# Differential attention: a filler's sums moved from VectorE to ScalarE and GpSimd, and one masked eviction for a row's last chunk

## The chip, the cores and the metric

The kernel runs on one core of one Trainium2 chip. A core has five engines with queues of their own: TensorE (PE in the profile; PEld are its weight loads), VectorE (DVE), ScalarE (ACT), GpSimd (POOL) and SyncE (SP, which issues nearly all DMAs here). The metric is the device time of one execution in microseconds. Lower is better. One execution was also taken with the hardware profiler; its trace is what the profile shows.

## The reference

Two transformer layers over 2048 tokens of width 1024, in float32. The first mixes three kinds of attention (six heads of stick-breaking attention, six of differential attention, four of attention to a memory of 256 tokens), the second has windowed attention and memory attention. Each layer ends in a gated product with `w_out` and a layer norm of `ALPHA * x + y`. The parts that the change touches:

```python
DEEPNORM_ALPHA = (2 * DEPTH) ** 0.25            # ALPHA in the kernel, the square root of 2

def _differential_attention(q, k, v, lam):
    ...
    s = jnp.einsum('bqhcd,bkhcd->bhcqk', qi, k) * scale
    causal = key_idx[None, :] <= q_idx[:, None]
    p = jax.nn.softmax(jnp.where(causal, s, NEG_BIG), axis=-1)
    a = p[:, :, 0] - lam * p[:, :, 1]
    return jnp.einsum('bhqk,bkhd->bqhd', a, v)

def _even_layer(x, mem, positions, ...):
    ...
    mixed = jnp.concatenate([sb_o, df_o, mem_o], axis=-1)
    y = (mixed * jax.nn.silu(gate)) @ w_out
    return _layer_norm(DEEPNORM_ALPHA * x + y, ln_g, ln_b)
```

## The kernel before

`run` goes through stages one after the other: `layer1_proj` (projections), `stick_breaking`, `differential`, `join` (the first layer's output product and norm), then `layer2_kv`, `layer2` and a last `out_proj`. Each stage has pools of SBUF tiles with a fixed number of buffers for each tag, and PSUM banks likewise. Matmuls of float32 are split into a high and a low part.

**Differential attention** works on 24 units: head pair `p` (3), half `k` (2), step `j` (4). `diff_parts` pairs a long row of query blocks with a short one, so that each unit has 17 blocks of 128 key columns: part `w = 0` with 9 to 16 of them, part `w = 1` with 1 to 8. For each of four score maps (`hc`: two heads, two maps each) `chunk` computes scores in chunks of up to 512 columns. A matmul writes a bank `psz` (three buffers), and VectorE evicts it into the SBUF tile `row` times `-scale`, and takes the minimum of a row on the way (`mn`, which the exponential needs). The last chunk of a part holds the diagonal block and needs the causal mask. One instruction, `tensor_tensor_reduce` (L779; CUSTOM_DVE_ANT_0 in the profile, ISA in the lists of order), adds the mask from the SBUF tile `mask`: zeros, then the triangle. The mask has two blocks of zeros, so that instruction reaches 384 columns. A last chunk of 512 columns is evicted in two pieces: 128 columns with the plain form (L777, TENSOR_SCALAR_CACHE_REDUCE), then 384 with the mask, starting from the first piece's minimum. That is so in part 0 where `j = 0` and in part 1 where `j = 3`: 3 x 2 x 2 x 4 = 48 chunks.

Then ScalarE takes exponentials in place (`exps`), VectorE forms the factors (L808, L812) and mixes two maps (`mix`, L819: `row` times a factor plus `row`, in three pieces). PE transposes the mixture (`pstp`), ScalarE copies the transposes into `wT` tiles (`tblocks`, a ring of seven buffers), and PE multiplies them with the values (`pspv`). `diff_norm` normalises a finished block of rows; its power (L895) and product (L897) run on GpSimd.

**The filler.** Beside all this, `filler` already computes five of the eight row blocks of the first layer's output product, in 32 blocks (two halves of columns, 16 blocks of rows). For each: `resid` loads 512 columns of `x` into `rx`, `split` splits the inputs (ScalarE, and GpSimd in L947), `products` issues 15 matmuls into the only bank `psmm`, and `finish` (L958) adds `ALPHA * x` to the product on VectorE and stores the sum to `rp`. The steps are spread evenly between the steps of attention. `join` loads `rp`, adds the last three row blocks of the product (L1063, in `out_proj`, with `alpha` None) and applies the norm.

**What sets the order.** In `differential` PE and ScalarE keep the program's order (`PinnedCore`). VectorE, GpSimd and SP are ordered by a scheduler that runs a timeline of its own when the kernel is built. On every engine, and on SP, the queue is then worked off in that order: what waits holds up what stands behind it.

Of the kernel before, what the change touches and what calls it, by code (L numbers as in the profile page):

```python
# [9 lines left out]
BF16 = mybir.dt.bfloat16  # L10
I32 = mybir.dt.int32
AF = mybir.ActivationFunctionType
ALU = mybir.AluOpType
# [53 lines left out]
class Net:  # L67
# [60 lines left out]
    def consts(self):  # L128
# [5 lines left out]

        self.mask = sb.tile([P, 3 * P + 2], BF16, name="mask")
        nc.vector.memset(self.mask[:, :2 * P], 0.0)
        nc.vector.memset(self.mask[:, 3 * P:], NEG)
        self.load_mask(2, 2)
        self.freq = sb.tile([P, 2], F32, name="freq")
# [406 lines left out]
    def stick_breaking(self):  # L546
# [33 lines left out]
        def scores(u):  # L580
            p, t, qi, c = u
            n, lo, hi = bounds(u)
            m, diag, s0 = hi - lo, hi == n, int(lo == 0)
            if qi == 3 and c == t:
                begin(p, t)
            if c == t:
                prs[p, t, qi] = [self.t("row", F32, [P, 2048]) for _ in range(2)]
                for hh in range(2):
                    nc.gpsimd.memset(prs[p, t, qi][hh][:, n - 1:n], 1.0)
            z = self.psum("z", [P, 2, 512])  # L590
            for hh in range(2):
                for k in range(2):
                    self.nc.tensor.matmul(z[:, hh, :m], qs[p, t][:, hh, k, qi * P:(qi + 1) * P], kv[p][0][hh][:, lo:hi], start=(k == 0),
                                          stop=(k == 1 and not diag))
                if diag:
                    self.nc.tensor.matmul(z[:, hh, m - P:m], self.identb, self.mask[:, 2 * P + 1:3 * P + 1], start=False, stop=True)
            zs[u] = z
# [144 lines left out]
    def diff_scores(self, unit, rows):  # L742
# [15 lines left out]
        def chunk(hc, w, c):  # L758
# [15 lines left out]
            before = mn[:, :1] if w and c else 3e38  # L774
            acc, n0 = mn[:, c:c + 1], max(0, m - 3 * P) if diag else m
            if n0:
                nc.vector.tensor_scalar(e[:, col + lo:col + lo + n0], z[:, :n0], -scale, before, ALU.mult, ALU.min, accum_out=acc)  # L777
            if diag:
                nc.vector.tensor_tensor_reduce(e[:, col + lo + n0:col + hi], z[:, n0:m], self.mask[:, 3 * P + n0 - m:3 * P], -scale,  # L779
                                               acc if n0 else before, ALU.add, ALU.min, acc)  # L780
            if w and c == 0:
# [130 lines left out]
    def filler(self):  # L912
# [43 lines left out]
        def finish(f):  # L956
            h, tb = blocks[f]
            self.nc.vector.scalar_tensor_tensor(res[f], res[f], ALPHA, res["ps"], ALU.mult, ALU.add)  # L958
            self.dma(self.rp[tb, :, 512 * h:512 * h + 512], res[f])
# [69 lines left out]

    def out_proj(self, w, msrc, spans, res, alpha, lng, lnb, tbs, ahead):  # L1030

# [19 lines left out]
        for k, tb in enumerate(tbs):  # L1051
# [7 lines left out]
            for h in range(2):  # L1059
                hs = slice(h * 512, h * 512 + 512)  # L1060
                ps = self.out_mm(mp, w, hs)
                if alpha is None:
                    nc.vector.tensor_add(r[:, hs], r[:, hs], ps)  # L1063
                else:
                    nc.vector.scalar_tensor_tensor(r[:, hs], r[:, hs], alpha, ps, ALU.mult, ALU.add)  # L1065
                nc.vector.bn_stats(st[:, 6 * h:6 * h + 6], r[:, hs])  # L1066
# [5 lines left out]
            nc.vector.scalar_tensor_tensor(r, r, mvr[:, 0:1], g, ALU.subtract, ALU.mult)  # L1072
            if alpha:
                for hs in (slice(0, 512), slice(512, 1024)):
                    nc.vector.scalar_tensor_tensor(r[:, hs], r[:, hs], rs, b[:, hs], ALU.mult, ALU.add)  # L1075
            else:
                nc.scalar.mul(r, r, rs)
                nc.gpsimd.tensor_add(r[:, :640], r[:, :640], b[:, :640])
                nc.vector.tensor_add(r[:, 640:], r[:, 640:], b[:, 640:])
            yield tb, r  # L1080

    def join(self, tail):
# [10 lines left out]
        raws[0] = self.t("big")  # L1093
        blocks = self.out_proj(w, self.m1, ((3, 6),), self.rp, None, i["ln_ge"], i["ln_be"], tbs, 2)

# [79 lines left out]
    def swa_scores(self, qb, head, qs, qcol, ks):  # L1175
# [12 lines left out]
        for hh in range(2):  # L1188
            nc.vector.tensor_tensor_reduce(e[:, hh, n0:], z[:, hh, n0:], self.mask[:, P + n0:3 * P], -1.0, self.nsink[:, head + hh:head + hh + 1],
                                           ALU.add, ALU.min, nmx[:, hh:hh + 1])  # L1190
# [227 lines left out]
    def run(self):  # L1418
        nc, dr, i = self.nc, self.dr, self.i
        with self.phase({"c2": 3, "sl": 2}, {}):  # L1420
# [17 lines left out]
            with self.phase({"big": 16}, {}):  # L1438
# [7 lines left out]
                with self.phase({"w": 4, "raw": 1, "cs": 2, "e": 4, "wT": 4, "kc": 2, "qs": 2, "vg": 4},  # L1446
                                {"mm": 2, "z": 3, "tp": 2, "pv": 1}):
                    self.load_mask(1, 1)
                    w = self.layer2()
                with self.phase({"gb": 2, "m": 3, "mp": 5, "rx": 6}, {"mm": 8}):  # L1450
                    tbs = [4 * t + q for t in (3, 0, 1, 2) for q in range(3, -1, -1)]
                    self.nc = PinnedCore(nc, self.tc, ("tensor",))
                    for tb, r in self.out_proj(w, self.m2, ((0, 8),), self.x2, ALPHA, i["ln_go"], i["ln_bo"], tbs, 3):
                        n = D // 2 if tb == tbs[-1] else D
                        for c in range(0, D, n):
                            self.dma(self.out[tb][:, c:c + n], r[:, c:c + n], nc.scalar if c else None)
# [68 lines left out]
```

## Time and profile before

| | us |
|---|---|
| median of 3 runs | 2526.95 |
| lowest and highest of them | 2522.09, 2529.95 |
| the profiled execution | 2526.36 |
| its span in the trace | 2524.5 |
| stage of differential attention, from the first score's eviction to the last one's | about 1050 to 1572 |

The profile lists instructions by line and tile, busy times of the engines in a stretch, and waits with what ended them. A line of a helper stands for all who call it: in `differential` PE and ScalarE are wrapped, and their instructions are under L57, so tiles tell them apart: `psz` scores, `psmm` the filler's product, `pstp` transposes, `pspv` products with the values. In waits, "A <- B" means that A's engine stood idle until B was done.

### The profile page before, as it was taken

Reading aid. Unit: us, or ns where it says so; the run is one execution under the profiler, and the core shown is the slowest. Engines: PE = TensorE matmul, PEld = TensorE weight load, DVE = VectorE, ACT = ScalarE, POOL = GpSimd, SP = SyncE. Lnnn points to the kernel's source line nnn. Section 1 sums busy time; section 2 is a strip of 40 time slices with the busy share of each in tenths; the row PEclk is TensorE's granted clock in tenths of the full one; section 3 lists DMA queues with packets and bytes.
Section 4 is the critical chain, followed back from the end, with each engine's and each line's share of the span. In section 5 each row is a group of like instructions: output and inputs, shape, how many; then the busy total and the mean of one; then the engine's idle time right before and its main releaser. Section 6 shows DMA issues by size and latency. Waiting matters only on the chain. (4 is left out here: it accounts for less than half of the span.)

```text
span 2524.5 us, 42315 instructions
## 1 busy us (share of the span) xinstructions
PE 2390.9 (95%) x15564; PEld 1939.1 (77%) x15564; DVE 1572.5 (62%) x3689; ACT 1262.1 (50%) x2459; POOL 939.6 (37%) x768
## 2 busy tenths in 40 slices
PE   9999999999999999889888998899999999999998
PEld 7888998888877777667666676688788777777887
DVE  4532223542278988799899998684313676777455
ACT  4432222232167877668677777443212777776100
POOL 0401003750068778511111111564511655534332
PEclk9999999999999999999999999999999999999999
DMA  8543222342433436734552431553324555532641
GB/s 282 196 142 126 72 87 90 130 138 79 135 87 94 108 85 133 160 90 109 128 134 72 112 87 54 197 183 108 95 89 116 162 151 153 145 102 98 200 149 60
DMA packets 199247, 311.60 MB, mean 123 GB/s; under 512 B 17920, under 2 KB 97280, under 8 KB 198528
## 3 DMA queue, kind: packets, MB, share of 16 engines
q1 hardware_dynamic: 198464, 307.83, 41.2%
q8 instruction: 124, 2.03, 0.4%
q10 hardware_dynamic: 576, 1.05, 0.1%
q14 instruction: 83, 0.68, 0.1%
HBM read 204.74 MB, written 104.07 MB: 122 GB/s over the span
## 5 line engine op out<-in xcount | busy, mean ns | idle before, releaser
L57 PE MATMUL psmm<-big,w 128*128 128x512 f32 x1680 | 413.2, 393 | 0.0
L57 PEld LDWEIGHTS psmm<-big,w 128*128 128x128 f32 x1680 | 305.3, 188 | 57.5
L57 ACT COPY wT<-pstp 128x512 f32<-128x512 f32 (+3 forms) x400 | 203.5, 526 | 188.9 <-PE pstp L57 182.9
L612 POOL TENSOR_TENSOR wb<-wb,row 128x512 f32<-128x512 f32 (+3 forms) x240 | 263.2, 1120 | 70.5 <-DVE row L57 45.4
L57 DVE TENSOR_TENSOR_SCAN row<-s,row,pszero 128x512 f32<-128x512 f32 (+5 forms) x240 | 254.1, 1104 | 38.2 <-ACT s L57 34.6
L254 PE MATMUL psmm<-big,w 128*128 128x512 f32 x1200 | 275.2, 389 | 0.0
L254 PEld LDWEIGHTS psmm<-big,w 128*128 128x128 f32 x1200 | 225.0, 188 | 47.0 <-issue 0.2
L57 PE MATMUL psmm<-big,mp 128*128 128x512 f32 x1056 | 246.0, 393 | 3.4 <-POOL big L1017 3.4
L57 ACT ACTIVATE row<-row,mn 128x2048 f32<-128x2048 f32 (+7 forms) x192 | 229.8, 1202 | 11.5 <-DVE mn L783 7.6
L57 PEld LDWEIGHTS psmm<-big,mp 128*128 128x128 f32 x1056 | 199.1, 190 | 45.4 <-POOL big L1017 3.8
L777 DVE TENSOR_SCALAR_CACHE_REDUCE row<-psz 128x512 f32<-128x512 f32 (+1 forms) x324 | 200.6, 639 | 16.0 <-PE psz L57 15.3
L947 POOL TENSOR_TENSOR mp<-mp,mp 128x640 fp32r<-128x640 f32 x32 | 54.2, 1693 | 347.4 <-ACT mp L57 274.9
L1236 DVE TENSOR_TENSOR c<-psmm,c 128x512 f32<-128x512 f32 x62 | 42.7, 691 | 219.2 <-ACT c L1235 219.1
L57 PE MATMUL psmm<-wo,mp 128*128 128x512 f32 x480 | 148.3, 421 | 6.3 <-ACT mp L57 5.5
L819 DVE SCALAR_TENSOR_TENSOR row<-row,tiny,row 128x128 f32<-128x128 f32 (+7 forms) x144 | 152.6, 1110 | 0.4
L209 POOL TENSOR_TENSOR w<-w,w 128x1024 fp32r<-128x1024 f32 x20 | 48.6, 2429 | 251.3 <-ACT w L208 147.0
L57 PE MATMUL pstp<-ident,wb 128*128 128x128 f32 x816 | 117.3, 276 | 22.8 <-DVE wT L57 15.3
L57 PE MATMUL pstp<-ident,row 128*128 128x128 f32 x816 | 130.4, 281 | 7.8 <-ACT wT L57 6.8
L1235 ACT ACTIVATE c<-psmm 128x512 f32<-128x512 f32 x62 | 36.8, 596 | 189.2 <-PE psmm L254 173.1
L57 PEld LDWEIGHTS pstp<-ident,wb 128*128 128x128 f32 x816 | 91.8, 141 | 43.7 <-POOL wb L612 27.0
L1193 ACT ACTIVATE e<-e,tiny 128x256 f32<-128x256 f32 (+1 forms) x192 | 94.7, 494 | 60.6 <-DVE e L1191 60.1
L57 PEld LDWEIGHTS pstp<-ident,row 128*128 128x128 f32 x816 | 99.4, 143 | 32.5 <-ACT wT L57 14.0
(236 smaller groups left out, 5009.9 us busy)
## 6 DMA issues: line engine op xcount, KB each, us to landing
silu<-c SPq DMA_DIRECT2D x54, 256.0 KB, 2.3
sl<-silu SPq DMA_DIRECT2D x54, 256.0 KB, 3.3
qs<-sbq SPq DMA_DIRECT2D x48, 256.0 KB, 5.3
cs<-rope SPq DMA_DIRECT2D x24, 512.0 KB, 4.2
kc<-k SPq DMA_DIRECT2D x36, 320.0 KB, 5.0
w<-in_we_dram SPq DMA_DIRECT2D x20, 512.0 KB, 3.7
raw<-in_wo_dram SPq DMA_DIRECT2D x20, 512.0 KB, 3.9
rx<-in_x_dram SPq DMA_DIRECT2D x32, 256.0 KB, 2.8
```

What stands on the lines that cost most here:

```text
L57: return self.tc.keep_in_program_order(f(*a, **k))
L209: eng.tensor_sub(lo[:, sl], raw[:, sl], hi[:, sl].bitcast(F32))
L254: self.nc.tensor.matmul(ps, w[a][:, c, :], self.xpart(t, c, b), start=(c == k == 0), stop=(c == 7 and k == 2))
L612: nc.gpsimd.tensor_mul(w[:, hh, :m], w[:, hh, :m], prr[:, lo:hi])
L777: nc.vector.tensor_scalar(e[:, col + lo:col + lo + n0], z[:, :n0], -scale, before, ALU.mult, ALU.min, accum_out=acc)
L819: self.nc.vector.scalar_tensor_tensor(x[:, lo:hi], y[:, lo:hi], cf[hh][:, w:w + 1], x[:, lo:hi], ALU.mult, ALU.add)
L947: self.nc.gpsimd.tensor_sub(ml, m, mh.bitcast(F32))
L1193: nc.scalar.activation(e[:, hh, ns:], e[:, hh, ns:], AF.Exp, bias=nmx[:, hh:hh + 1], scale=-1.0, accum_out=s[:, hh:hh + 1])
L1235: nc.scalar.activation(sg, ps, AF.Sigmoid)
L1236: nc.vector.tensor_mul(sg, ps, sg)
```

## The change

Two edits in the stage of differential attention, and what follows from them.

1. The mask gets a third block of zeros. The last chunk of a part is evicted in one masked instruction whatever its width, and the plain form does only whole chunks of 512 columns off the diagonal. The other users of the mask shift their columns by one block.
2. `finish` no longer runs on VectorE. ScalarE multiplies the product in PSUM by `1 / ALPHA` into a `wT` tile, and GpSimd adds that to `x`. So `rp` holds the sum divided by `ALPHA`, and `join` multiplies by it: its `out_proj` now takes the form with `alpha`, and a new argument `final` tells which norm follows. The scratch that is reserved for DMAs issued at run time is halved from 2048 to 1024.

```diff
-        self.mask = sb.tile([P, 3 * P + 2], BF16, name="mask")
-        nc.vector.memset(self.mask[:, :2 * P], 0.0)
-        nc.vector.memset(self.mask[:, 3 * P:], NEG)
-        self.load_mask(2, 2)
+        self.mask = sb.tile([P, 4 * P + 2], BF16, name="mask")
+        nc.vector.memset(self.mask[:, :3 * P], 0.0)
+        nc.vector.memset(self.mask[:, 4 * P:], NEG)
+        self.load_mask(2, 3)
...
             before = mn[:, :1] if w and c else 3e38
-            acc, n0 = mn[:, c:c + 1], max(0, m - 3 * P) if diag else m
-            if n0:
-                nc.vector.tensor_scalar(e[:, col + lo:col + lo + n0], z[:, :n0], -scale, before, ALU.mult, ALU.min, accum_out=acc)
+            acc = mn[:, c:c + 1]
             if diag:
-                nc.vector.tensor_tensor_reduce(e[:, col + lo + n0:col + hi], z[:, n0:m], self.mask[:, 3 * P + n0 - m:3 * P], -scale,
-                                               acc if n0 else before, ALU.add, ALU.min, acc)
+                nc.vector.tensor_tensor_reduce(e[:, col + lo:col + hi], z[:, :m], self.mask[:, 4 * P - m:4 * P], -scale, before, ALU.add, ALU.min, acc)
+            else:
+                nc.vector.tensor_scalar(e[:, col + lo:col + hi], z, -scale, before, ALU.mult, ALU.min, accum_out=acc)
...
         def finish(f):
             h, tb = blocks[f]
-            self.nc.vector.scalar_tensor_tensor(res[f], res[f], ALPHA, res["ps"], ALU.mult, ALU.add)
+            part = self.t("wT")
+            self.nc.scalar.mul(part, res["ps"], 1.0 / ALPHA)
+            self.nc.gpsimd.tensor_add(res[f], res[f], part)
             self.dma(self.rp[tb, :, 512 * h:512 * h + 512], res[f])
...
-    def out_proj(self, w, msrc, spans, res, alpha, lng, lnb, tbs, ahead):
+    def out_proj(self, w, msrc, spans, res, alpha, final, lng, lnb, tbs, ahead):
...
-                if alpha is None:
-                    nc.vector.tensor_add(r[:, hs], r[:, hs], ps)
-                else:
-                    nc.vector.scalar_tensor_tensor(r[:, hs], r[:, hs], alpha, ps, ALU.mult, ALU.add)
+                nc.vector.scalar_tensor_tensor(r[:, hs], r[:, hs], alpha, ps, ALU.mult, ALU.add)
...
-            if alpha:
+            if final:
...
-        blocks = self.out_proj(w, self.m1, ((3, 6),), self.rp, None, i["ln_ge"], i["ln_be"], tbs, 2)
+        blocks = self.out_proj(w, self.m1, ((3, 6),), self.rp, ALPHA, False, i["ln_ge"], i["ln_be"], tbs, 2)
...
-    nc = _bacc.Bacc("TRN2", target_bir_lowering=False, num_devices=1, dynamic_dma_scratch_size=2048)
+    nc = _bacc.Bacc("TRN2", target_bir_lowering=False, num_devices=1, dynamic_dma_scratch_size=1024)
```

PE's order stays as it is. The orders of the other engines, as the two programs are built (line, operation, output, inputs, columns), at three places of the stage. First VectorE, where it evicts the scores of the last map (`hc` = 3) of a unit with `j = 0`. Before:

```order
L808 RECIPROCAL tiny_11437<-tiny_11177 128x2
L812 SCALAR_TENSOR_TENSOR tiny_11437<-s_2083_11176,nlam,tiny_11437 128x2
L777 TENSOR_SCALAR row_11359,mn_11360<-psz_11380 128x128
L777 TENSOR_SCALAR row_11359,mn_11360<-psz_11385 128x512
L819 SCALAR_TENSOR_TENSOR row_11188<-row_11249,tiny_11437,row_11188 128x640
L819 SCALAR_TENSOR_TENSOR row_11188<-row_11249,tiny_11437,row_11188 128x768 x2
L779 ISA row_11359,mn_11360<-psz_11380,mask,mn_11360 128x384
L779 ISA mn_11360 128x1
```

And now, where line numbers are those of the changed kernel (one lower here, with the masked form at L777 ahead of the plain one at L779):

```order
L807 RECIPROCAL tiny_11441<-tiny_11183 128x2
L777 ISA row_11364,mn_11365<-psz_11385,mask 128x512
L777 ISA mn_11365 128x1
L811 SCALAR_TENSOR_TENSOR tiny_11441<-s_2090_11182,nlam,tiny_11441 128x2
L779 TENSOR_SCALAR row_11364,mn_11365<-psz_11389 128x512
L782 TENSOR_REDUCE mn_11365<-mn_11365 128x1
L818 SCALAR_TENSOR_TENSOR row_11194<-row_11254,tiny_11441,row_11194 128x640
L818 SCALAR_TENSOR_TENSOR row_11194<-row_11254,tiny_11441,row_11194 128x768 x2
```

The bank `psz` of the last chunk was evicted in two pieces, with another bank's eviction and three pieces of mixing between them. It is now evicted in one, ahead of the mixing.

ScalarE a little before that, where it copies transposes (`wT<-pstp`) and takes exponentials (`row<-row,mn`). Before:

```order
L57 COPY wT_11259<-pstp_11254 128x512
L57 COPY wT_11273<-pstp_11268 128x512
L57 ACTIVATE row_11188,s_2083_11176<-row_11188,mn_11189 128x1536
L57 ACTIVATE row_11188,s_2083_11176<-row_11188,mn_11189 128x640
L57 COPY wT_11313<-pstp_11308 128x512
L57 COPY wT_11330<-pstp_11325 128x512
```

And now:

```order
L57 COPY wT_11264<-pstp_11259 128x512
L57 COPY wT_11278<-pstp_11273 128x512
L57 ACTIVATE row_11194,s_2090_11182<-row_11194,mn_11195 128x1536
L57 ACTIVATE row_11194,s_2090_11182<-row_11194,mn_11195 128x640
L57 ACTIVATE wT_11292<-psmm_11122 128x512
L57 COPY wT_11319<-pstp_11314 128x512
L57 COPY wT_11336<-pstp_11331 128x512
```

A product (`wT<-psmm`) stands ahead of the two copies of transposes.

GpSimd, from a filler's block to a block that `diff_norm` normalises. Before:

```order
L947 TENSOR_TENSOR mp_11509<-mp_11445,mp_11508 128x640
L947 TENSOR_TENSOR mp_11708<-mp_11617,mp_11707 128x640
L895 TENSOR_TENSOR tiny_11722<-tiny_11722,mhalf 128x8
L897 TENSOR_TENSOR c_2199_11644<-c_2199_11644,tiny_11722 128x512
L947 TENSOR_TENSOR mp_11919<-mp_11828,mp_11918 128x640
```

And now:

```order
L946 TENSOR_TENSOR mp_11515<-mp_11449,mp_11514 128x640
L959 TENSOR_TENSOR rx_11498<-rx_11498,wT_11677 128x512
L946 TENSOR_TENSOR mp_11716<-mp_11623,mp_11715 128x640
L894 TENSOR_TENSOR tiny_11730<-tiny_11730,mhalf 128x8
L896 TENSOR_TENSOR c_2208_11650<-c_2208_11650,tiny_11730 128x512
L959 TENSOR_TENSOR rx_11699<-rx_11699,wT_11862 128x512
L946 TENSOR_TENSOR mp_11929<-mp_11836,mp_11928 128x640
```

One addition (L959) follows each block's subtraction, and some stand behind a power (L895, now L894).

More of the change, by code (lines that the diff above doesn't have):

```diff
@@ L595, in scores @@
                 if diag:
-                    self.nc.tensor.matmul(z[:, hh, m - P:m], self.identb, self.mask[:, 2 * P + 1:3 * P + 1], start=False, stop=True)
+                    self.nc.tensor.matmul(z[:, hh, m - P:m], self.identb, self.mask[:, 3 * P + 1:4 * P + 1], start=False, stop=True)
             zs[u] = z
@@ L1188, in swa_scores @@
         for hh in range(2):
-            nc.vector.tensor_tensor_reduce(e[:, hh, n0:], z[:, hh, n0:], self.mask[:, P + n0:3 * P], -1.0, self.nsink[:, head + hh:head + hh + 1],
+            nc.vector.tensor_tensor_reduce(e[:, hh, n0:], z[:, hh, n0:], self.mask[:, 2 * P + n0:4 * P], -1.0, self.nsink[:, head + hh:head + hh + 1],
                                            ALU.add, ALU.min, nmx[:, hh:hh + 1])
@@ L1447, in run @@
                                 {"mm": 2, "z": 3, "tp": 2, "pv": 1}):
-                    self.load_mask(1, 1)
+                    self.load_mask(1, 2)
                     w = self.layer2()
@@ L1452, in run @@
                     self.nc = PinnedCore(nc, self.tc, ("tensor",))
-                    for tb, r in self.out_proj(w, self.m2, ((0, 8),), self.x2, ALPHA, i["ln_go"], i["ln_bo"], tbs, 3):
+                    for tb, r in self.out_proj(w, self.m2, ((0, 8),), self.x2, ALPHA, True, i["ln_go"], i["ln_bo"], tbs, 3):
                         n = D // 2 if tb == tbs[-1] else D
```

## The prediction

> **What bounds the kernel now.** The page comes first: span and busy times.
>
> ```profile
> span 2524.5 us, 42315 instructions
> PE 2390.9 (95%) x15564; PEld 1939.1 (77%) x15564; DVE 1572.5 (62%) x3689; ACT 1262.1 (50%) x2459; POOL 939.6 (37%) x768
> ```
>
> Over the whole span PE is the bound and DVE is at 62%, so taking work from DVE should be worth nothing. That average hides the stages. The view of busy time by stretch, cut where differential attention begins, where its last score is evicted and where the next layer begins, shows the one that differs (columns: length, then busy us and count for PE, PEld, DVE, ACT, POOL; granted clock; DMA share and GB/s).
>
> ```profile
> core 0: us, PE busy (x) PEld busy (x) DVE busy (x) ACT busy (x) POOL busy (x), PEclk, DMA share, GB/s
> 1050.00:1572.00 522.00, 452.69 (x3272) 347.23 (x3267) 475.13 (x1460) 371.39 (x669) 84.06 (x51) 0.96 0.39 105
> 1572.00:1700.00 128.00, 116.92 (x687) 95.61 (x686) 98.50 (x162) 54.83 (x89) 72.78 (x49) 0.97 0.56 188
> ```
>
> From 1050 to 1572 us DVE is busy 475 of 522 us (91%), more than PE (453). ACT has 71%, POOL 16%. Every diagonal chunk and every filler sum lies here. The view of waits, restricted to 1050 to 1580 us, says who stood for whom (us in total, times, longest).
>
> ```profile
> PE psz L57 <- DVE row L777: 33.5, 53, 3.1
> PE psz L57 <- DVE mn L779: 17.0, 18, 2.1
> DVE row L777 <- PE psz L57: 15.3, 26, 1.6
> DVE tiny L808 <- ACT row L57: 19.2, 9, 7.2
> ACT wT L57 <- PE pstp L57: 111.3, 106, 6.8
> PEld pstp L57 <- ACT wT L57: 12.6, 18, 1.6
> PE pstp L57 <- ACT wT L57: 7.1, 11, 1.3
> POOL tiny L895 <- DVE tiny L891: 63.5, 7, 14.8
> SPq L113 <- DVE rx L958: 65.9, 16, 7.8
> ```
>
> PE stood 33.5 + 17.0 = 50.5 us for DVE to evict a score bank, most of its 69 idle us. DVE stood 15.3 us for PE and 19.2 us for an exponential of ACT. So the stage has two engines that wait for each other in turn through three score banks, DVE more often the late one.
>
> **The change part by part.** Merging the last chunk. The rows by form give each duration (us in total, mean ns after the bar).
>
> ```profile
> L777 DVE TENSOR_SCALAR_CACHE_REDUCE row<-psz 128x128 f32<-128x128 f32 x36 | 10.2, 283 | 2.0 <-PE psz L57 2.0
> L777 DVE TENSOR_SCALAR_CACHE_REDUCE row<-psz,mn 128x128 f32<-128x128 f32 x12 | 4.1, 342 | 0.1
> L777 DVE DVE_READ_ACCUMULATOR row<-psz 128x1 f32 x324 | 26.5, 82 | 0.0
> L779 DVE CUSTOM_DVE_ANT_0 row<-psz,mask,mn 128x384 f32<-128x384 f32 x60 | 36.7, 612 | 1.0 <-PE psz L57 0.3
> L779 DVE CUSTOM_DVE_ANT_0 row<-psz,mask 128x384 f32<-128x384 f32 x36 | 19.9, 553 | 1.2 <-PE psz L57 1.0
> L779 DVE CUSTOM_DVE_ANT_0 row<-psz,mask 128x256 f32<-128x256 f32 x36 | 15.0, 416 | 0.0
> L779 DVE CUSTOM_DVE_ANT_0 row<-psz,mask 128x128 f32<-128x128 f32 x36 | 10.2, 283 | 1.4 <-PE psz L57 1.4
> L958 DVE SCALAR_TENSOR_TENSOR rx<-rx,psmm 128x512 f32<-128x512 f32 x32 | 21.9, 683 | 2.9 <-PE psmm L57 2.6
> ```
>
> The 36 + 12 = 48 instructions of 128 columns are the first halves of the 512-wide diagonal chunks. They go (10.2 + 4.1 = 14.3 us), with 48 accumulator reads of 82 ns (3.9 us) and 48 masked halves of 612 ns (29.4 us). In comes a masked form of 512 columns, which no row shows: 283, 416 and 553 ns for 128, 256 and 384 columns grow by 135 a step, which gives 688; a start value read from memory adds 612 - 553 = 59, so 747. 36 x 688 + 12 x 747 = 33.7 us. DVE saves 14.3 + 3.9 + 29.4 - 33.7 = **13.9 us**. If the fourth step cost nothing the saving were 20, if it cost twice as much 7.
>
> The merge also frees a score bank earlier. The timeline around 1290 us shows what stood between two halves of one chunk.
>
> ```profile
> 1289.89 0.28 DVE L777 TENSOR_SCALAR_CACHE_REDUCE row<-psz 128x128 f32<-128x128 f32 x1
> 1290.10 3.53 DVE L819 SCALAR_TENSOR_TENSOR row<-row,tiny,row 128x384 f32<-128x384 f32 x3
> 1293.62 0.60 DVE L779 CUSTOM_DVE_ANT_0 row<-psz,mask,mn 128x384 f32<-128x384 f32 x1
> 1294.37 0.91 PE L57 MATMUL psz<-kd,qd 128*128 128x512 f32 x2 [1.32 <-DVE tiny L808]
> ```
>
> The bank was held from 1289.89 to 1294.2 us, three mixing instructions lay in it, and PE stood 1.32 us at the next score. A merged eviction is done before or begun after them. I take 2 us for all 48 (some two such waits), between 0 and 8.
>
> The sums. The 32 sums of L958 leave DVE: **21.9 us**. They become 32 ScalarE products that read PSUM and 32 GpSimd additions. Nearest rows, three of later stages, and the evictions of the `wT` ring in this one:
>
> ```profile
> L1162 ACT ACTIVATE c<-psmm 128x512 f32<-128x512 f32 x24 | 14.1, 589 | 8.2 <-PE psmm L57 8.0
> L1167 POOL TENSOR_TENSOR c<-c,c 128x512 f32<-128x512 f32 x23 | 29.6, 1288 | 1.8
> L1063 DVE TENSOR_TENSOR rx<-rx,psmm 128x512 f32<-128x512 f32 x29 | 19.4, 670 | 8.5 <-PE psmm L57 7.4 <-issue 1.1
> L57 ACT COPY wT<-pstp 128x512 f32<-128x512 f32 x158 | 90.8, 588 | 96.7 <-PE pstp L57 95.4 <-PE psz L57 0.6
> ```
>
> ACT gets 32 x 0.589 = 18.8 us and goes from 71% to 75%. Its queue is in program order; behind a product stand evictions of transposes, for which PE waits, and exponentials, for which DVE waits. Those waits are now 12.6 + 7.1 + 19.2 = 38.9 us for 371 us of ACT work, a tenth, so 18.8 us cost 1.9; the ends are 0 and 18.8. The product needs PE's last matmul of the block and may hold ACT there, but ACT already stands 111.3 us for PE's transposes, and both queues keep one order.
>
> POOL gets 32 x 1.288 = 41.2 us, and has the room: 84 of 522. Each product takes one of the seven `wT` buffers until its addition is done, and an addition can stand behind L895, which waited 63.5 us in 7 times. With 158 full evictions in 522 us (3.3 us each) the ring needs up to 23 us for a turn, less by the narrower ones; a wait of 9 us on the mean is covered, and nothing is taken. Without the cover ACT's evictions, and behind them PE, would stand for up to the longest, 14.8 us, at some of the 7 places. The store of a sum now follows the addition: 0.589 + 1.288 against 0.683, 1.2 us later. On SP the loads of later blocks and queries stand behind it; they stood 65.9 us for L958 already and are issued a step ahead. Nothing is taken for it. In the join 32 additions (670) become the form of L958 (683): 0.4 us, if none hides.
>
> But the additions meet DVE's mixing (L819), which also reads two tiles of SBUF: first its rows and POOL's by form, then one meeting in the timeline.
>
> ```profile
> L819 DVE SCALAR_TENSOR_TENSOR row<-row,tiny,row 128x512 f32<-128x512 f32 x6 | 4.5, 747 | 0.1
> L819 DVE SCALAR_TENSOR_TENSOR row<-row,tiny,row 128x768 f32<-128x768 f32 x18 | 17.8, 1012 | 0.0
> L819 DVE SCALAR_TENSOR_TENSOR row<-row,tiny,row 128x640 f32<-128x640 f32 x18 | 20.6, 1171 | 0.0
> L819 DVE SCALAR_TENSOR_TENSOR row<-row,tiny,row 128x704 f32<-128x704 f32 x12 | 13.8, 1187 | 0.0
> L819 DVE SCALAR_TENSOR_TENSOR row<-row,tiny,row 128x896 f32<-128x896 f32 x18 | 23.5, 1331 | 0.0
> L819 DVE SCALAR_TENSOR_TENSOR row<-row,tiny,row 128x960 f32<-128x960 f32 x12 | 18.2, 1543 | 0.0
> L947 POOL TENSOR_TENSOR mp<-mp,mp 128x640 fp32r<-128x640 f32 x31 | 52.6, 1698 | 347.4 <-ACT mp L57 274.9 <-PE pstp L57 35.2 <-PE psz L57 25.8
> L897 POOL TENSOR_TENSOR c<-c,tiny 128x512 f32<-128x512 f32 x10 | 15.3, 1532 | 0.6
> ```
>
> ```profile
> 1395.63 1.99 POOL L947 TENSOR_TENSOR mp<-mp,mp 128x640 fp32r<-128x640 f32 x1 [15.15 <-ACT mp L57]
> 1396.12 2.11 DVE L819 SCALAR_TENSOR_TENSOR row<-row,tiny,row 128x576 f32<-128x576 f32 x1
> ```
>
> A mixing of 704 columns takes longer on the mean than one of 768, so widths don't explain these means. From 512 and 768 columns (747, 1012) a step of 64 is worth 66 ns; by that 576 columns take 813 ns, and the one that began inside a subtraction of POOL took 2.11 us: 1.30 lost. The same line gives 879, 946, 1144 and 1211 for 640, 704, 896 and 960; their means lie above it by 292, 241, 187 and 332 ns, or 5.3 + 2.9 + 3.4 + 4.0 = 15.6 us. POOL was busy 52.6 + 15.3 = 67.9 us in those two lines, so each us of POOL cost DVE 0.23. For 41.2 us of additions that is 9.5; four widths of L819 are counted alone, so I take **12 us**, between 0 and 41.2 (each addition paid in full).
>
> The Trainium skill, "SBUF — State Buffer", section "Who interferes with whom", says that a VectorE instruction with two SBUF inputs contends with a GpSimd instruction that reads SBUF, as an exclusive lock, and that the later one blocks fully. The trace agrees (1.30 us lost beside a row of 1.99), and an instruction like L958, with one input in PSUM, is by that rule free of it. "Perfetto Trace Analysis", section "Optimizing Scalar/DVE Operations", warns that moving work between these two engines might not help for this reason; by it the 21.9 us would come back as up to 41.2, and the sum would end on the slow rival below.
>
> Sum: DVE loses 13.9 + 21.9 - 12 = 23.8 us of work. How much of that shortens the stage? All, if DVE set each moment; a quarter, if PE's order, with 453 us of its own, took over soon. PE's 50.5 us for DVE against DVE's 34.5 for PE and ACT lie between; I take **half, 11.9**. The profiled execution took 2526.36 us (span 2524.5; the runs' median is 2526.95, so it stands for them): 2526.4 - 11.9 - 2 + 1.9 + 0.4 = 2514.8, **about 2515**.
>
> **The rivals.** *The relief falls off the path*: PE and ACT become the bound, a quarter counts: -6 + 2.3, 2523. For it: PE is at 453 of 522, and DVE, whose order a scheduler redoes, already waits for ACT. Against: PE's 50.5 us.
>
> *The lock takes it back* (slower): additions fall into the runs of three mixings, and the evictions queued behind these are the ones PE stands for, so each hit counts in full while the relief counts half: -(35.8 / 2) - 2 + 1.9 + 0.4 = -17.6, plus 1.29 per hit. All 32 hit: 2550. It becomes slower by over 7.6 us from 20 hits of 32. For it: 1396.12. Against: 15.6 us at 1.3 are some 12 hits among 41.
>
> *Everything counts*: hardly a hit (5 us) and DVE on the path throughout: 35.8 - 5 = 31 off, 2496. For it: 91%. Against: DVE's own 34.5 us of waits.
>
> **How the numbers follow.** Forecast (2504 to 2519) 0.48; off the path (2519 to 2534) 0.31; lock 0.11; everything 0.10. A measurement of this kernel can tell 0.3% (7.6 us) from no change. Faster 0.48 + 0.10 = 0.58, within 0.31, slower 0.11. The range 2501 to 2532 leaves out most of the last two cases and the outer ends of the costs above.
>
> **What would show it.** In the changed profile: 48 rows fewer at 128 columns and a masked 512 form near 690; DVE's busy time in the stage down from 475 to about 451; L819's means above the line by 12 us more; PE's wait for score evictions down from 50.5 to some 40, and the stage shorter by 11 to 14. Wrong would be: L819 up by 25 us or more, PE waiting for ACT's `wT` by 10 us more, or DVE standing longer for exponentials behind products.

## The result, and the profile after

| | before | after |
|---|---|---|
| median of 4 runs each, same chip, us | 2528.45 | 2511.28 |
| lowest and highest | 2522.09, 2531.32 | 2508.77, 2512.29 |
| profiled execution (span) | 2526.36 (2524.5) | 2510.68 (2508.9) |

The ratio is 0.9935, with a 95% interval of 0.9922 to 0.9949: the change makes the kernel faster by 0.5 to 0.8%. The forecast was 2515 (2501 to 2532). By the medians 17.2 us were gained, by the profiled executions 15.7, against the 11.6 of the sum.

The page of the changed kernel, span and busy times:

```profile
span 2508.9 us, 42155 instructions
PE 2378.9 (95%) x15564; PEld 1931.9 (77%) x15564; DVE 1547.0 (62%) x3561; ACT 1274.4 (51%) x2491; POOL 983.0 (39%) x800
```

VectorE has 128 instructions fewer and GpSimd 32 more. The view of busy time by stretch, for the stage up to its last score's eviction, which stood at 1572 us before and stands at 1554 now (columns as in the prediction):

```profile
1050.00:1554.00 504.00, 437.93 (x3233) 336.83 (x3229) 447.45 (x1329) 380.44 (x696) 125.59 (x82) 0.97 0.41 106
```

DVE fell from 475.13 to 447.45 us of work, the stage from 522 to 504 us. The new rows by form, 1050 to 1565 us (us in total, mean ns of one):

```profile
L777 DVE CUSTOM_DVE_ANT_0 row<-psz,mask 128x512 f32<-128x512 f32 x36 | 24.7, 686 | 3.6 <-PE psz L57 3.5
L777 DVE CUSTOM_DVE_ANT_0 row<-psz,mask,mn 128x512 f32<-128x512 f32 x12 | 8.9, 741 | 0.2
L57 ACT ACTIVATE wT<-psmm 128x512 f32<-128x512 f32 x31 | 18.5, 595 | 2.9 <-PE psmm L57 2.9
L959 POOL TENSOR_TENSOR rx<-rx,wT 128x512 f32<-128x512 f32 x31 | 41.9, 1351 | 297.0 <-ACT wT L57 286.0 <-PE psz L57 11.1
```

The prediction's prices were 688, 747, 589 and 1288 ns. Mixing, first on the page of before, then on that of after:

```profile
L819 DVE SCALAR_TENSOR_TENSOR row<-row,tiny,row 128x128 f32<-128x128 f32 (+7 forms) x144 | 152.6, 1110 | 0.4
```

```profile
L818 DVE SCALAR_TENSOR_TENSOR row<-row,tiny,row 128x128 f32<-128x128 f32 (+7 forms) x144 | 148.6, 1083 | 0.6
```

It did not get 12 us longer; it got 4 us shorter. The same line on the pages of two kernels from the experiments below, first of number 9 (no additions on GpSimd), then of number 10 (the changed kernel with additions of one column):

```profile
L819 DVE SCALAR_TENSOR_TENSOR row<-row,tiny,row 128x128 f32<-128x128 f32 (+7 forms) x144 | 148.0, 1076 | 0.4
```

```profile
L818 DVE SCALAR_TENSOR_TENSOR row<-row,tiny,row 128x128 f32<-128x128 f32 (+7 forms) x144 | 145.2, 1060 | 0.6
```

So mixing fell without any addition too (why is not shown), and the additions gave back 3.4 us of it. The waits of after, 1050 to 1565 us (us in total, times, longest):

```profile
PE psz L57 <- DVE row L779: 27.9, 48, 2.0
PE psz L57 <- DVE mn L777: 12.5, 10, 2.3
PE psmm L57 <- ACT wT L57: 12.6, 1, 12.6
PE pstp L57 <- ACT wT L57: 10.3, 15, 1.7
DVE row L779 <- PE psz L57: 24.8, 36, 1.7
DVE row L777 <- PE psz L57: 12.3, 18, 1.4
DVE tiny L807 <- ACT row L57: 16.7, 8, 8.9
ACT mp L57 <- DMA mp<-m: 13.0, 1, 13.0
```

PE's waits for score evictions went from 50.5 to 40.4 us. Those of DVE for PE's scores went the other way, to 24.8 + 12.3 = 37.1 us; before, they were 15.3 and, in the masked form (1050 to 1580 us):

```profile
DVE row L779 <- PE psz L57: 2.6, 6, 1.0
```

One wait is new: PE stood once, for 12.6 us, for a product of ScalarE. It is in the opening of the stage, and the timeline there shows its cause.

```profile
1061.19 3.98 SPq L113 DMA_DIRECT2D qd<-dfq  x4
...
1065.26 0.98 SPq L113 DMA_DIRECT2D mp<-m  x2
...
1070.05 0.72 ACT L57 CAST mp<-mp 128x640 fp32r<-128x640 f32 x1 [12.98 <-DMA mp<-m]
...
1075.05 0.57 ACT L57 ACTIVATE wT<-psmm 128x512 f32<-128x512 f32 x1
...
1075.68 1.65 PE L57 MATMUL psmm<-wo,mp 128*128 128x512 f32 x3 [12.64 <-ACT wT L57]
```

ScalarE's cast waited 12.98 us for a block `mp` whose loads stand on SP behind eight loads of queries (`qd`; four of them are shown). The product (`wT<-psmm`) stands behind that cast on ScalarE, and behind three exponentials that follow the cast (not shown); while it does not come, the only `psmm` bank stays full.

**Where the time went.** Every kernel here issues the same 15,564 matmuls, the first 11,000 of them in the same order, so each trace can be cut at the same matmuls: the *opening* from the 7,000th to the 7,200th, and the *main stretch* from there to the 10,500th, just behind the stage. Before, then after:

```profile
1052.56:1113.39 60.83, 46.09 (x201) 32.78 (x201) 51.08 (x159) 34.31 (x57) 11.42 (x6) 0.92 0.60 155
1113.39:1605.05 491.66, 431.97 (x3305) 334.25 (x3301) 433.78 (x1314) 351.25 (x640) 78.44 (x48) 0.97 0.38 104
```

```profile
1052.58:1114.01 61.43, 42.91 (x201) 31.59 (x201) 45.84 (x145) 36.31 (x63) 17.52 (x12) 0.89 0.59 148
1114.01:1591.08 477.07, 424.50 (x3304) 328.53 (x3301) 413.80 (x1200) 361.00 (x667) 116.29 (x75) 0.98 0.40 108
```

In the main stretch DVE lost 20.0 us of work, and the stretch became 14.6 us shorter, 0.73 of it. In the opening DVE lost 5.2 us, and nothing was gained (0.6 us longer).

Not all of the gain is waiting. In the main stretch PE's busy time for the same matmuls fell from 431.97 to 424.50 us, at a granted clock of 0.97 and then 0.98; so of the 14.6 us, 7.5 are PE's busy time and 7.1 its idle time. Within one kernel the time goes with the granted clock: of the runs of number 8 below, one took 2515.05 us at 0.991 and one 2529.58 at 0.985. The four runs of the changed kernel were granted 0.989 to 0.991, the 17 of the kernel before beside numbers 1 to 4 0.983 to 0.989. At the same 0.990, three runs of the kernel before took 2520.48 to 2522.16 us and two of the changed one 2508.77 and 2511.89: some 11 us apart, where the medians are 17 apart. Whether the change raises the granted clock, or the clock differed for another reason, is not shown.

Behind the main stretch, which the edits hardly touch, the 14 traces take between 917.3 and 919.9 us. Differences of 2 to 3 us in a stretch of one execution are therefore not resolved.

### The profile page after: what moved, and what is told of

Same layout as the page of the kernel before. It is cut to its first block, busy times and chain, and to the rows that moved or that the text cites. A ratio compares the mean times of both kernels' runs of the same rounds, so it can differ in the third digit from the quotient of the medians.

```text
span 2508.9 us, 42155 instructions
## 1 busy us (share of the span) xinstructions
PE 2378.9 (95%) x15564; PEld 1931.9 (77%) x15564; DVE 1547.0 (62%) x3561; ACT 1274.4 (51%) x2491; POOL 983.0 (39%) x800
## 3 DMA queue, kind: packets, MB, share of 16 engines
q10 hardware_dynamic: 576, 1.05, 0.1%
## 5 line engine op out<-in xcount | busy, mean ns | idle before, releaser
L779 DVE TENSOR_SCALAR_CACHE_REDUCE row<-psz 128x512 f32<-128x512 f32 x288 | 190.4, 685 | 25.5 <-PE psz L57 24.8
L959 POOL TENSOR_TENSOR rx<-rx,wT 128x512 f32<-128x512 f32 x32 | 43.2, 1349 | 310.7 <-ACT wT L57 299.6
L57 PE MATMUL psmm<-wo,mp 128*128 128x512 f32 x480 | 145.5, 415 | 12.6 <-ACT wT L57 12.6
L818 DVE SCALAR_TENSOR_TENSOR row<-row,tiny,row 128x128 f32<-128x128 f32 (+7 forms) x144 | 148.6, 1083 | 0.6
```

The lines of the kernel that those rows point to most:

```text
L57: return self.tc.keep_in_program_order(f(*a, **k))
L779: nc.vector.tensor_scalar(e[:, col + lo:col + hi], z, -scale, before, ALU.mult, ALU.min, accum_out=acc)
L818: self.nc.vector.scalar_tensor_tensor(x[:, lo:hi], y[:, lo:hi], cf[hh][:, w:w + 1], x[:, lo:hi], ALU.mult, ALU.add)
L959: self.nc.gpsimd.tensor_add(res[f], res[f], part)
```

## The experiments

All kernels keep PE's order, but for 16 matmuls of 7 and 11 that lie behind the main stretch. The halved scratch was not tried alone; number 1 has it and number 2 has not. Every ratio is to runs of the kernel before on the same chip. Opening and main stretch are those of the one profiled execution; DVE and POOL are their busy times in the main stretch.

| kernel | median us | ratio, 95% interval | opening | main | DVE | POOL |
|---|---|---|---|---|---|---|
| before | 2526.9 to 2529.0 | 1 | 60.83 | 491.66 | 433.78 | 78.44 |
| changed | 2511.28 | 0.9922 to 0.9949 | 61.43 | 477.07 | 413.80 | 116.29 |
| 1 merge only | 2518.21 | 0.9938 to 0.9966 | 63.10 | 481.46 | 426.84 | 79.26 |
| 2 sums moved only | 2517.27 | 0.9936 to 0.9964 | 64.67 | 480.63 | 420.60 | 115.93 |
| 3 before, no sums | 2530.67 | 0.9996 to 1.0015 | 71.99 | 478.95 | 413.48 | 81.20 |
| 4 changed, queries later | 2508.11 | 0.9903 to 0.9931 | 59.36 | 475.39 | 413.86 | 115.66 |
| 5 changed, additions twice | 2523.41 | 0.9976 to 0.9996 | 63.94 | 484.30 | 421.99 | 151.59 |
| 6 changed, and zeros written | 2512.35 | 0.9929 to 0.9955 | 60.45 | 477.62 | 415.27 | 144.24 |
| 7 as 3, queries later | 2529.10 | 0.9996 to 1.0017 | 71.04 | 478.78 | 415.27 | 81.03 |
| 8 before, queries later | 2523.97 | 0.9974 to 1.0001 | 57.92 | 490.48 | 433.46 | 78.86 |
| 9 before, sums over 1 column | 2511.91 | 0.9922 to 0.9960 | 60.43 | 478.85 | 416.92 | 79.70 |
| 10 changed, additions over 1 column | 2508.42 | 0.9909 to 0.9948 | 61.35 | 474.98 | 409.19 | 86.81 |
| 11 merge, sums over 1 column | 2509.74 | 0.9911 to 0.9954 | 60.54 | 476.76 | 412.72 | 80.21 |
| 12 changed, products and additions over 1 column | 2508.38 | 0.9913 to 0.9958 | 60.89 | 472.38 | 410.85 | 85.46 |

**1 and 2: one edit at a time.** The changed kernel with the sum of before (1; `join` has its form of before again), and the kernel before with the sums of the changed one (2).

```diff
-            part = self.t("wT")
-            self.nc.scalar.mul(part, res["ps"], 1.0 / ALPHA)
-            self.nc.gpsimd.tensor_add(res[f], res[f], part)
+            self.nc.vector.scalar_tensor_tensor(res[f], res[f], ALPHA, res["ps"], ALU.mult, ALU.add)
...
```

> The kernel before with the first edit alone: the last chunk of 512 columns is evicted in one masked instruction; the sums stay on VectorE. Theory A (relief of VectorE, about half of it on the path): from one start to the next the two pieces take about 0.21 + 0.53 us and the merged one 0.61, so 48 x 0.13 to 0.2 = 6 to 10 us of VectorE work go, and the time falls by 3 to 6 us (about 2523). Theory B (the score bank that is freed earlier is the main gain): the time falls by more than VectorE's work does, by 10 us or more (2518 or less).

> The kernel before with the second edit alone: the filler's sums go to ScalarE and GpSimd, the last chunk is still evicted in two pieces. Theory A: 32 x 0.60 = 19 us leave VectorE, the mixing loses little to the additions, and the time falls by 9 to 13 us (about 2517). Theory B: by 7 us or less, since the rest of the 17 us came from the banks.

The main stretches of 1 and of 2:

```profile
1114.88:1596.34 481.46, 428.23 (x3304) 331.81 (x3301) 426.84 (x1226) 350.78 (x640) 79.26 (x48) 0.97 0.39 106
```

```profile
1117.82:1598.45 480.63, 427.61 (x3304) 330.59 (x3301) 420.60 (x1288) 361.81 (x667) 115.93 (x75) 0.97 0.40 107
```

By the medians number 1 lies 10.8 us below the kernel before and number 2 11.7: theory B for the merge, theory A for the sums. On DVE the edits add up: 6.9 and 13.2 us less work, 20.0 together. On the path they do not: 10.2 and 11.0 us alone, 14.6 together. The merge alone gains more than the work that it takes from DVE; of its 10.2 us, 3.7 are PE's busy time (431.97 to 428.23).

**3 and 7: the sums left out.** `rp` gets `x` alone, so the projections' part of the sum is missing. In 7 the queries' loads were also to go behind two blocks of the filler, by the edit of 4.

```diff
-            self.nc.vector.scalar_tensor_tensor(res[f], res[f], ALPHA, res["ps"], ALU.mult, ALU.add)
```

> The kernel before without the filler's sums: VectorE no longer adds them, nobody does, and x alone is stored (this leaves the first five row blocks out of the first layer's output). It is the second edit at no cost on ScalarE and GpSimd. If the products on ScalarE and the additions on GpSimd cost next to nothing, it lies within 3 us of the run with the second edit alone. If their place in the queues or the lock costs what I had priced (2 us for ScalarE, half of 12 us for the lock), it is 6 to 8 us faster than that run.

> The kernel before with the filler's 32 sums left out (x alone is stored, so the projections' part of that sum is missing from the output), and with the first unit's eight query loads put on SP behind the loads of the third and fourth block of the filler. Theory of the opening: without the sums VectorE is relieved by 19 us, of which some 12 to 16 shorten the stage, and the run without this reordering (2530.7) lost as much again in the stage's first 60 us, where ScalarE's cast waits for a block whose loads stand behind the queries': now 2512 to 2518, 11 to 16 us below the kernel before. Rival, the sums are worth nothing to the path: 2525 or more.

Opening and main stretch of 3:

```profile
1059.10:1131.09 71.99, 49.63 (x201) 35.61 (x201) 49.42 (x153) 34.57 (x58) 9.40 (x6) 0.81 0.46 110
1131.09:1610.04 478.95, 427.24 (x3305) 330.64 (x3301) 413.48 (x1288) 349.51 (x640) 81.20 (x48) 0.97 0.36 96
```

The relief is there (20.3 us of DVE, 12.7 us of the main stretch), but the opening is 11.2 us longer, and 6.5 more are lost ahead of it (1052.56 became 1059.10; PE stood once 5.6 us there for ScalarE). Number 3 came out 13 us above number 2, where both of its theories had it beside or below that run. The waits of 3 in the opening, 1045 to 1115 us:

```profile
ACT mp L57 <- DMA mp<-m: 14.6, 1, 14.6
PE psmm L57 <- ACT mp L57: 14.2, 2, 9.9
ACT mp L57 <- DMA sl<-silu: 10.2, 1, 10.2
```

Without a sum to wait for, loads of `x` and stores of `rp` that belong later move to the front of SP, and the block's own loads come after them. The timeline of 7 shows it, and that its edit did not do what was meant: four query loads still stand ahead of the third block's load, and the other four, at 1078.08, ahead of the fourth's at 1082.54.

```profile
1036.55 3.31 SPq L113 DMA_DIRECT2D rp<-rx  x3
1040.31 2.81 SPq L113 DMA_DIRECT2D rx<-in_x_dram  x3
1043.80 2.49 SPq L113 DMA_DIRECT2D rp<-rx  x3
...
1070.64 4.67 SPq L57 DMA_DIRECT2D qd<-dfq  x4
1076.47 0.91 SPq L57 DMA_DIRECT2D mp<-m  x2
```

So neither run is a test of the sums alone. Number 7 came out where its rival said, for a reason that was not the rival's.

**9: the sums over one column.** This keeps the instruction and its waits, and with them the opening of before.

```diff
-            self.nc.vector.scalar_tensor_tensor(res[f], res[f], ALPHA, res["ps"], ALU.mult, ALU.add)
+            self.nc.vector.scalar_tensor_tensor(res[f][:, :1], res[f][:, :1], ALPHA, res["ps"][:, :1], ALU.mult, ALU.add)
```

> The kernel before with the filler's 32 VectorE sums over one column of 512 (511 columns of that sum are missing from the output); the instruction, its waits and the store behind it stay, so that the order of loads in the stage's first 60 us is that of the kernel before. VectorE is relieved of 31 x (0.60 - 0.1) = 16 us from start to start, and no other engine gets work. Theory of the opening (the run without the sums lost its gain there): 9 to 13 us below the kernel before, 2514 to 2518. Rival, the sums are not worth anything to the path: within 3 us of the kernel before.

```profile
1112.72:1591.57 478.85, 430.86 (x3305) 333.98 (x3301) 416.92 (x1314) 350.40 (x640) 79.70 (x48) 0.96 0.39 107
```

The opening stayed (60.43 against 60.83 us), and now the relief shows: 16.9 us of DVE became 12.8 us of the main stretch (11.7 of them idle time of PE), and the run is some 15 us below the kernel before, more than was expected. With the order of loads the loss of 3 and 7 is gone. The relief is not all that changed, though: the scheduler also put some 130 of VectorE's 3,689 instructions elsewhere in its queue.

**11: the same with the merge.** Number 1 with the sums over one column.

> The kernel before with the merged eviction and with the sums over one column on VectorE (511 columns of that sum are missing from the output): both reliefs and no new work on ScalarE and GpSimd. If the reliefs add up, 9 to 10 us of the merge and what the run with one column alone gained: 2505 or less. If each takes a part of the same waits (PE is busy 453 of the stage's 522 us), less than the sum, and near the changed kernel: 2507 to 2512; the distance to the changed kernel is then what ScalarE's products and GpSimd's additions cost in all.

```profile
1113.79:1590.55 476.76, 426.95 (x3305) 331.86 (x3301) 412.72 (x1226) 350.19 (x640) 80.21 (x48) 0.96 0.39 108
```

The merge took 4.2 us more from DVE, but only 2.1 us more from the stretch; by the medians it added 2 us, which these runs do not resolve. Alone it had brought 10.2. So each edit alone brings most of what both bring, as the second theory had it. The distance to the changed kernel, 1.5 us by the medians, is within both intervals.

**5 and 6: more work on GpSimd.** In 5 each addition is done twice; in 6 zeros are written twice behind it. The orders of the other engines are those of the changed kernel.

```diff
             self.nc.gpsimd.tensor_add(res[f], res[f], part)
+            self.nc.gpsimd.tensor_add(part, res[f], part)
```

```diff
             self.nc.gpsimd.tensor_add(res[f], res[f], part)
+            self.nc.gpsimd.memset(part, 0.0)
+            self.nc.gpsimd.memset(part, 0.0)
```

> The changed kernel, in which GpSimd does each of the filler's 32 additions twice: the second, of two tiles of SBUF, into a buffer that nobody reads, so the output stays. The order of every other engine is that of the changed kernel; POOL gets 31 x 1.35 = 42 us more in the stage. The prediction's rate (0.23 us of VectorE's mixing for each us of POOL): mixing 9.6 us longer than the changed kernel's 148.6, time up by half of it, 5 us, to 2516. Theory of the place (an addition begins where ScalarE's product ends, and that is seldom within a run of mixing, 2 times in 31): mixing up by less than 4 us, time within 3 us of 2511.3. Ring theory (a wT buffer is held 1.35 us longer, and ScalarE then waits for one): ScalarE's waits for POOL up by 5 us or more, whatever mixing does.

> The changed kernel, in which GpSimd, behind each of the filler's 32 additions, writes zeros twice into the wT buffer that the addition has read: nothing reads them, so the output stays. POOL is busy longer and holds the buffer longer, but reads no SBUF in that time. The lock between two readers of SBUF: no rise of mixing over the changed kernel's 148.6 us (within 1.5 us), time within 2 us of 2511.3. If any work on POOL slows mixing, or the buffer's hold costs, this run rises as the one with the second addition does.

The main stretches of 5 and of 6:

```profile
1117.81:1602.11 484.30, 427.07 (x3304) 330.19 (x3301) 421.99 (x1200) 361.22 (x667) 151.59 (x102) 0.97 0.39 107
```

```profile
1116.17:1593.79 477.62, 425.57 (x3305) 329.44 (x3301) 415.27 (x1200) 361.52 (x668) 144.24 (x129) 0.97 0.40 108
```

Second additions: POOL 35.3 us more, DVE 8.2 us more with the same 1,200 instructions, the stretch 7.2 us longer (and the opening 2.5), the median 12 us up. Zeros: POOL 28.0 us more, DVE 1.5, the stretch 0.6, the median 1 us up. So what costs here is not GpSimd's work but its reading of SBUF (with the zeros mixing stays at 148.5 us, as the theory of the lock had it), and 8.2 / 35.3 = 0.23 is the prediction's rate. It does not fall on mixing alone. Rows of the changed kernel by form, 1045 to 1580 us, and the same of 5:

```profile
L811 DVE SCALAR_TENSOR_TENSOR tiny<-s,nlam,tiny 128x2 f32<-128x2 f32 x48 | 15.2, 317 | 0.5
L889 DVE SCALAR_TENSOR_TENSOR tiny<-s 128x8 f32<-128x8 f32 x10 | 2.3, 231 | 0.0
```

```profile
L811 DVE SCALAR_TENSOR_TENSOR tiny<-s,nlam,tiny 128x2 f32<-128x2 f32 x48 | 17.8, 372 | 0.5
L889 DVE SCALAR_TENSOR_TENSOR tiny<-s 128x8 f32<-128x8 f32 x10 | 4.8, 481 | 0.0
```

These two gave 2.6 and 2.5 us of it; mixing went from 148.6 to 152.7 on the page:

```profile
L818 DVE SCALAR_TENSOR_TENSOR row<-row,tiny,row 128x128 f32<-128x128 f32 (+7 forms) x144 | 152.7, 1111 | 0.6
```

The theory of the place and the ring's both missed (time was to stay within 3 us; ScalarE had no new wait for POOL); the rate hit on DVE, and its half on the path was too little.

**10 and 12: the new operations cut.** The changed kernel with the addition over one column (10), and with the product over one column as well (12).

```diff
-            self.nc.gpsimd.tensor_add(res[f], res[f], part)
+            self.nc.gpsimd.tensor_add(res[f][:, :1], res[f][:, :1], part[:, :1])
```

> The changed kernel with GpSimd's 32 additions over one column (the rest of that sum is missing from the output); ScalarE's products stay whole. The order of PE, VectorE and ScalarE is that of the changed kernel. It takes 31 x 1.2 = 37 us from GpSimd. The prediction's price (0.23 us of VectorE for each us of GpSimd): 9 us of VectorE, 5 to 9 us below the changed kernel. Price by the changed kernel's own trace (6 meetings, 3.4 us): 2 to 4 us below it, 2507 to 2509. Rival, no price: within 1.5 us of 2511.3.

> The changed kernel with both the product on ScalarE and the addition on GpSimd over one column (the rest of that sum is missing from the output). Against the run whose addition alone is cut, it takes 32 x (0.595 - 0.23) = 12 us from ScalarE. The prediction's price of the products (a tenth of ScalarE's added time): 1 to 2 us below that run. Rival, the products hold up the evictions of transposes and the exponentials behind them in full: 6 us or more below it.

```profile
1111.91:1586.89 474.98, 427.73 (x3304) 332.22 (x3301) 409.19 (x1200) 360.66 (x667) 86.81 (x74) 0.96 0.40 109
```

```profile
1112.10:1584.48 472.38, 422.00 (x3304) 328.05 (x3301) 410.85 (x1200) 351.48 (x666) 85.46 (x74) 0.97 0.40 109
```

The additions cost DVE 413.80 - 409.19 = 4.6 us and the stretch 2.1; by the medians it is 2.9 us, but the intervals overlap, so the time alone does not establish it. That is the price by the changed kernel's own trace (2 to 4 us), not the one by the prediction's rate (5 to 9). Cutting the products too changed the median by nothing and this stretch by 2.6 us, in which PE's busy time fell by 5.7 and its idle time rose: their price is small, and not resolved. The 6 us or more of the rival, in which they hold ScalarE's queue up in full, did not appear.

**4 and 8: the opening.** In the changed kernel (4) and in that of before (8) the eight query loads of the first unit go to SP behind the loads of two of the filler's blocks.

```diff
...
-            if j % 2 == 0:
+            if j % 2 == 0 and unit != (0, 0, 0):
...
+                if unit == (0, 0, 1) and hc == 3:
+                    self.load_dq(0, 0, 1, Pinned(self.nc.sync, self.tc))
...
-                    self.dma(m[:, k:k + b - a], self.m1[a:b, :, tb * P:(tb + 1) * P].rearrange("f p t -> p f t"))
+                    self.dma(m[:, k:k + b - a], self.m1[a:b, :, tb * P:(tb + 1) * P].rearrange("f p t -> p f t"), Pinned(self.nc.sync, self.tc) if f in (2, 3) else None)
```

> The changed kernel with the loads of the second query tiles (qd) of the first unit moved behind the filler's loads of its third and fourth block in SP's queue. In the changed kernel ScalarE stood 13.0 us for such a load at the opening of the stage, with a product behind it for which PE stood 12.6 us. If SP's order makes that wait, both waits fall to 5 us or less and the time falls by 5 to 10 us against the changed kernel (2501 to 2506). If the opening is set by the exponentials behind the wait anyway, the waits move and the time stays within 3 us of 2511.

> The kernel before with the same reordering on SP alone, nothing else: what the opening is worth in it. Theory of the opening: the changed kernel gained 3 to 4 us by it, the kernel before waits less there (11.8 us of ScalarE's cast for its block against 13.0, 5.5 of PE behind it against 12.6): 1 to 4 us below the kernel before, 2525 to 2528. Rival, the reordering costs as much at the queries as it gains at the blocks: within 1 us or above.

The waits of 4 in the opening, 1045 to 1115 us:

```profile
ACT mp L57 <- DMA mp<-m: 7.6, 1, 7.6
PE psmm L57 <- ACT wT L57: 2.1, 2, 1.2
```

The cast's wait fell from 13.0 to 7.6 us, PE's from 12.6 to 2.1. The opening became 2.1 us shorter in 4 and 2.9 in 8; the medians fell by 3 us in both. In 4 that is less than the 5 to 10 us that were expected, and the cast's wait stayed above the expected 5 us; in 8 it is as expected, but the interval reaches 1, so the gain is not resolved. Number 4 is faster than the kernel before (ratio 0.9917) and the fastest full computation here; that it also beats the changed kernel is likely, not certain, since the intervals overlap a little (0.9903 to 0.9931 against 0.9922 to 0.9949).

## Why the prediction was right

The mechanism was right: the stage was bound by DVE's turn with PE, both edits took work from it, and some half of that came off the time. Several terms were mis-sized, and their errors offset each other: merge, sums and lock measure 7.2, 19.0 and 4.6 us by the runs that take them apart, 21.6 in all, where the sum had 13.9, 21.9 and 12, 23.8 in all. That the total came out so near is luck.

- **The merge's saving on DVE, 13.9 us, was too large.** The prices of the two masked forms were right to 6 ns, yet number 1 shows 6.9 us in the main stretch and 0.3 in the opening (51.08 to 50.82). The working added up durations, and these overlap. In the timeline of after an eviction starts 0.61 us after the one ahead of it, while the rows give 0.69 for it and 0.08 for its read:

```profile
1062.40 0.69 DVE L779 TENSOR_SCALAR_CACHE_REDUCE row<-psz 128x512 f32<-128x512 f32 x1
1063.01 0.08 DVE L779 DVE_READ_ACCUMULATOR row<-psz 128x1 f32 x1
1063.01 0.69 DVE L779 TENSOR_SCALAR_CACHE_REDUCE row<-psz 128x512 f32<-128x512 f32 x1
```

  From start to start, the first half cost 0.21 us (1289.89 to 1290.10 in the prediction's timeline), and each instruction that goes saves less than its row says. The Trainium skill, "Perfetto Trace Analysis", section "Optimizing Scalar/DVE Operations", says of the fixed overhead of an instruction that its profiled latency is about twice the engine's busy time, since the write-acknowledgement half overlaps with the next instruction; in these rows too the end of one, 0.08 us, lies within the next.
- **The sums' saving, 21.9 us, was nearly right**: number 9 gives 16.9 + 2.1 = 19.0 us with a column still computed.
- **The lock, 12 us given back, was too large.** It is 4.6 us by number 10, where 29.5 us of POOL's work went from the stretch (116.29 to 86.81): a rate of 0.16. The rate of 0.23 from before, which holds for the second additions (number 5), gave 9.5; rounding that up to 12 made it worse. The mechanism itself, two readers of SBUF, is what 5 and 6 show. The Trainium skill, "SBUF — State Buffer", section "Who interferes with whom", says that a GpSimd instruction that only writes SBUF does not contend; number 6 agrees (1.5 us of DVE for 28.0 of POOL).
- Together DVE was to lose 23.8 us; over opening and main stretch it lost 484.87 - 459.63 = 25.2 us (both stretches together, before and after). The 3.6 us beyond the 21.6 are not accounted for.
- **The half that counts** came out as 14.0 of 25.2 us (552.49 to 538.50 for both stretches), 0.56. But this is a mean of two places: 0.73 in the main stretch, where the two engines alternate, and nothing in the opening, where the waits for loads on SP lie. And it is not waiting alone, as the prediction had it: 7.5 of the 14.6 us of the main stretch are PE's busy time. At the same granted clock some 11 us were gained, 0.45 of the 25.2. The rival in which a quarter counts (2523) is 12 us away, and the one in which all does (2496) 15.
- **The bank freed earlier, 2 us**: alone, the merge brought 10.2 us of the main stretch for 6.9 of DVE, where number 9 got 12.8 for 16.9. That speaks for a bank worth some 5 us (10.2 less 0.76 x 6.9). On top of 9 it added 2.1 us for 4.2, which does not. What of it is the bank stays open, and so does what sets the bound after the first 13 us of relief; that DVE stood 37.1 us for PE's scores in the changed kernel, where it was 17.9, fits a turn that has become nearly even.
- **The products, 1.9 us**, and **the ring of `wT`, nothing**: 10 against 12 gives 0 by the medians and 2.6 by the main stretch, neither resolved, and 6, which holds each buffer 1.05 us longer (two rows of 527 ns), cost 1 us at most.
- What was to be seen: the rows of 512 columns, PE's waits (40.4 for "some 40") and DVE's busy time (447 for "about 451") came as told; mixing 12 us longer did not. The stage is 18 us shorter to its last eviction, against 11 to 14; at the 10,500th matmul it is 14.0. One of the signs named as wrong did appear, PE waiting for ScalarE's `wT` by 10 us more: 12.6 us, in one place. The opening is only 0.6 us longer: the kernel before also stood there (5.5 us of PE behind the same cast), and while PE's idle time rose from 14.7 to 18.5 us, its busy time fell from 46.1 to 42.9. Number 4 took 2.1 us off the opening by moving the loads. DVE did not stand longer for exponentials (16.7 us against 19.2), though its longest such wait, 8.9 us, lies in the opening.
- One reading was a little wide: not every sum lies in the stretch from 1050 to 1572 us. The last of the 32 starts at 1579.5.

The rival in which the lock takes it back needed 20 hits of 32. Number 5 shows that the lock's hits do count on the path, nearly one for one (7.2 us of stretch for 8.2 of DVE), so that rival was sized rightly; it fell because the additions that the change makes cost DVE 4.6 us in all, some 4 meetings at 1.3, and not 20.

## What to carry to other kernels

Cut the trace at the same instruction before and after, and look at each stretch: a share like "half of the relief counts" can be three quarters in one place and nothing in another. Put PE's busy time and its granted clock beside the waits before you credit a gain to them. Price what goes from start to start, not by the durations in the rows, and give GpSimd work that reads two tiles of SBUF only against a count of the two-input VectorE instructions beside it. To measure what an instruction is worth, shrink it and keep its waits; taking it out altogether can reorder the loads behind it and hide the gain.

## What was not expected of the hardware

The length of a VectorE instruction does not shield it from GpSimd. In number 5 a factor of two columns, 0.22 us at 1073.39 in the changed kernel, took as long as the subtraction that had begun before it:

```profile
1105.82 1.56 POOL L946 TENSOR_TENSOR mp<-mp,mp 128x640 fp32r<-128x640 f32 x1 [0.98 <-ACT mp L57]
1105.89 1.51 DVE L811 SCALAR_TENSOR_TENSOR tiny<-s,nlam,tiny 128x2 f32<-128x2 f32 x1
```

Mixing waits behind that factor, so 1.3 us are lost before a run of mixing has begun. The prediction counted hits on mixing only; short instructions, L811 ahead of it and L889 in the norm, took as much in number 5 (2.6 + 2.5 us against 4.1).
